# Stepping four side lanes of an RWKV-7 recurrence together at every eighth step of a projection stream, and storing another branch's gates first

## The chip, the cores and the metric

The kernel runs on one core of one Trainium2 chip. The metric is device time in microseconds (us) of one execution, the median of several runs. The engines are PE (TensorE: matmuls, and the weight loads that the profile lists as PEld), DVE (VectorE), ACT (ScalarE), POOL (GpSimd) and SP (SyncE, which here only issues DMAs). Each engine works through its own queue in order and waits on semaphores of the others.

## The reference

One decoder layer is computed for a prompt of 512 tokens and 8 samples of 8 tokens, 576 tokens in all, with a model width of 1024:

```
xn = RMSNorm(x)
proj = xn @ w_in            # 1024 x 13440: conv, rwkv, memory and gate columns
y_conv = B * conv3(C * h) * silu(g_conv)
y_rwkv = RWKV7(shifted r, k, v, decay, icl) * silu(g_rwkv)
y_mem  = softmax(q K_mem^T / sqrt(d)) V_mem * silu(g_mem)
merged = sum_i sigmoid(m_i) * (y_i @ w_branch_i)
y = RMSNorm_final(x + merged @ w_out)
```

The recurrence of RWKV-7 (16 heads with a state of 64 x 64) goes, step by step, as

```
sa = S kk
S  = S * w - sa (kk * a)^T + v k^T
o  = S r
```

and the layer also returns the memory keys and values and the new states.

## The kernel before

Everything is laid out with features on the 128 partitions and the 576 tokens in the free dimension, as two halves of 288. A weight tile of 1024 x 128 is loaded as two DMAs on SP, split by ACT (`wh`, L99) and POOL (`wl`, L93) into a high and a low part, and multiplied by the high and low parts of the activations. One such projection is 48 matmuls on L245, a pair for each of 24 steps. Its result stands in a PSUM tile `m`, of which there are two.

These projections are the **main stream**. It runs through 25 tiles for the recurrence's inputs, 32 for the convolution and 8 for the queries; then through gate tiles; and, after the recurrence, through the branch products (`w_br`) and what gates are left, and the output projection (L1284).

The recurrence runs beside it, on **side lanes**. A lane is a queue of Python generators. `drive` takes one step of the main stream (one pair of matmuls, here called a step), adds one to `TICK[0]`, and then steps each lane once, in the order chain, post, merge, invert, prepare. A generator that yields n is let alone for n steps and goes on at the next one. PE's order is the order in which this code issues (the pool is told so with `manual_schedule`), so a lane's step puts its matmuls between two pairs of the stream. The order on the other engines is set by the framework's scheduler.

The recurrence is done for eight pairs of heads, p = 0 to 7, in chunks of 64 tokens:

- `prep` (prepare lane) makes decays and scaled keys (L578, L579, L599), the chunk matrices (L633, L642), and at the end the bonus term (L676, L677). It yields 5, 5, 5, 3, 3, 5, 8, 6, 6 and 16 between its parts.
- `invert` (invert lane) solves a triangular system on DVE, two small operations per step for 31 steps, and writes it back over DRAM (`sco` to `msk`).
- `merge` (merge lane) transposes (L720, L727, L818, L819) and applies the inverse (L796, L803, L755, L756, L768), with yields of 4, 5, 5, 7, 5 and 6. It may go on from its first part only `READY` = 92 steps after the inversion.
- `chain` (chain lane) carries the state over the nine chunks (L869, L887, L882, L843), with a yield of 7 on either side of each half chunk.
- `post` (post lane) updates the samples' states (L916) and normalizes the output (L942, L946), with yields of 17, 1, 12 and 15.

All of these but the chain take their PSUM from one pool, tile name `s`, **with two buffers for all lanes** (`stile`, here called a slot). A slot is free again when ACT or DVE has read it out. `prep` takes two slots at once for L578/L579, for L633, for L642 and for L676/L677; merge takes two at L755/L756 and one elsewhere; post takes one at L916 and two at L942/L946.

The recurrence is longer than the work that the stream has for it. When convolution and queries are done, `filler` goes on with gate tiles of branches 1 and 2 (`EARLY`, L403), until all lanes are empty. Such a gate goes through tanh and is stored in DRAM (L506); `branch` later fetches it (L1018) in place of a projection. At the end of the program `prep_lane` loads and splits the output weights (`wout`) during branch 1, one eighth every 28 steps.

Of the kernel before, what the change touches and what calls it, by code (L numbers as in the profile page):

```python
# [17 lines left out]
TICK = [0]  # L18
# [67 lines left out]
def hybrid_step(ctx, tc, x_nat, x_t, mem_t, w_in, w_br, w_mk, w_mv, w_o, kc, vc, swkv,  # L86
# [5 lines left out]
    def tt(e, out, a, b, op):  # L92
        e.tensor_tensor(out=out, in0=a, in1=b, op=op)  # L93
# [4 lines left out]
    def act(out, in_, f=AF.Copy, **k):  # L98
        S.activation(out, in_, f, **k)  # L99
# [133 lines left out]
    def mm(src, rh=None, rl=None, n=HT, ps=None, parts=None):  # L233
        rh, rl = (xh, xl) if rh is None else (rh, rl)
        if parts is None:
            parts = wload(src.rearrange("p k f -> p (k f)"))
        nh = 1 if n == 256 else 2
        if ps is None:
            ps = pm.tile([128, 2, 512], F32, name="m")
        for k in range(8):  # L240
            h, l = parts[k // 4]
            f = slice(k % 4 * 128, k % 4 * 128 + 128)
            for i, (a, b) in enumerate(((h, rh), (h, rl), (l, rh))):
                for hf in range(nh):
                    TE.matmul(ps[:, hf, :n], a[:, f], b[:, k, hf * n:hf * n + n],  # L245
                              start=(k == 0 and i == 0), stop=(k == 7 and i == 2))
                if nh == 2 or i:
                    yield
        return ps
# [4 lines left out]

    class Lane:
        def __init__(self):
            self.q, self.cur, self.wait = [], None, 0

        def busy(self):
            return self.cur is not None or bool(self.q)  # L260
# [1 line left out]
        def step(self):  # L262
            if self.wait > 0:
                self.wait -= 1
                return
            if self.cur is None:
                if not self.q:
                    return
                self.cur = self.q.pop(0)
            try:  # L270
                self.wait = next(self.cur) or 0
            except StopIteration:
                self.cur, self.wait = None, 0

    chain_lane, post_lane, prep_lane, inv_lane, mrg_lane = (Lane() for _ in range(5))
    lanes = [chain_lane, post_lane, mrg_lane, inv_lane, prep_lane]

    def drive(main):
        for _ in main:
            TICK[0] += 1  # L280
            for ln in lanes:
                ln.step()
# [117 lines left out]
    def etile(tag, dt=F32, **k):  # L400
        return el.tile([128, T], dt, name="e" + tag, tag=tag, **k)

    EARLY = [(i, j) for i in (1, 2) for j in range(8)]  # L403
    gates = {}
    QT = ("r", "k", "A", "B", "C", "D", "E1", "F")
    qt = []
# [1 line left out]
    def queries():  # L408
        for j in range(8):
            ps = yield from mm(w_in[WQ + j])  # L410
            t = etile(QT[j])
            act(v3(t), m3(ps), scale=1.0 / 16)
            qt.append(t)
            yield "tile"

    with ExitStack() as rctx:
# [81 lines left out]
        def early_gates():  # L498
            for i, j in EARLY:
                ps = yield from mm(w_in[WM[i] + j])  # L500
                t = cvp.tile([128, T], F32, name="c")
                act(v3(t), m3(ps), AF.Tanh, scale=0.5)
                d = gates[i, j] = drp.tile([128, T], F32, name="gate%d%d" % (i, j), bufs=1)
                S.dma_start(out=d, in_=t)
                yield "tile"
# [9 lines left out]
        def lora():  # L515
            act(blkr, cc("blk"))
            ps = yield from mm(w_in[WP + 24])

            lor, swp = etile("A"), etile("B")
            shift(ps, 24, lor)  # L520
            act(lor[up], lor[up], AF.Tanh)
            S.dma_start(out=swp[dn], in_=lor[up])
            S.dma_start(out=swp[up], in_=lor[dn])
            stacks(lx, lor, swp)
            for o, (a, b) in enumerate(((lor, swp), (swp, lor))):
                tt(V, xlo[o][up], a[up], lx[o][up].bitcast(F32), ALU.subtract)
                tt(V, xlo[o][dn], b[dn], lx[o][dn].bitcast(F32), ALU.subtract)
# [25 lines left out]
        def proj(p, i):  # L553
            ps = yield from mm(w_in[WP + 8 * i + p])
            if i < 2:
                t = etile("rk"[i])
                shift(ps, 8 * i + p, t)
            else:
                t = fvas[p]
                shift(ps, 8 * i + p, t[:, :, 0, :], flat=False)  # L560
            got[p, i] = t
# [388 lines left out]
        def rwkv_main():  # L950
            yield from lora()
            n = [0, 0]

            def filler():
                es = early_gates()

                def one():
                    for x in es:
                        yield x
                        if x == "tile":  # L960
                            return
                    yield
                    yield "tile"

                for j in range(8):
                    while j >= 6 and want[0] < 8:
                        yield from one()
                    yield from conv(j)
                yield from queries()
                while any(ln.busy() for ln in lanes) or n[1] < 8:  # L970
                    yield from one()

            cg = filler()
            more = True
            while True:
                p = n[0] // 2
                if n[1] in fvas:
                    yield from proj(n[1], 2)
                    n[1] += 1
                elif p < 8 and want[0] >= p:  # L980
                    yield from proj(p, n[0] % 2)
                    n[0] += 1
                    if n[0] % 2 == 0:
                        prep_lane.q.append(prep(p))
                elif more:
                    more = False
                    for x in cg:
                        if x == "tile":
                            more = True
                            break  # L990
                        yield
                elif any(ln.busy() for ln in lanes) or n[1] < 8:
                    yield
                else:
                    return

        drive(rwkv_main())

    S.dma_start(out=o_conv, in_=cvo)
    S.dma_start(out=o_shift, in_=sho)  # L1000
# [13 lines left out]
    def branch(i, yh, yl, first=False, merged=None):  # L1014
        for j in range(8):
            if (i, j) in gates:
                th = etile("v", bufs=2)
                DMA.dma_start(out=th, in_=gates[i, j])  # L1018
            else:
                ps = yield from mm(w_in[WM[i] + j])  # L1020
                th = etile("v", bufs=2)
                act(v3(th), m3(ps), AF.Tanh, scale=0.5)
            ps = yield from mm(w_br[8 * i + j], yh, yl)
            if first:
                stt(v3(acc[:, j, :]), v3(th), 1.0, m3(ps), ALU.add, ALU.mult)
                continue
            stt(v3(th), v3(th), 1.0, m3(ps), ALU.add, ALU.mult)
            if merged is None:
                tt(G, acc[:, j, :], acc[:, j, :], th, ALU.add)
            else:  # L1030
                mgh, mgl = merged
                tt(G, th, acc[:, j, :], th, ALU.add)
                act(mgh[j], th, scale=0.5)
                stt(mgl[:, j, :], th, 0.5, mgh[j].bitcast(F32), ALU.mult, ALU.subtract)
# [204 lines left out]
    def wout(n, lag):  # L1239
        def place(pool, *parts):  # L1240
            r = []
            for tag, m in parts:
                t = pool.tile([128, m, 512], F32R, name="wo" + tag, tag=tag)
                r += [t[:, i, :] for i in range(m)]
            return r

        if n == 0:
            h, l = place(keep, *((t, 2) for t in SLOTS)), place(keep, ("s4", 7), ("s4b", 1))
        else:
            h, l = place(late, ("yh", 8)), place(late, ("yl", 8))  # L1250
        wo.append((h, l))
        for k in range(8):
            w = wp.tile([128, 512], F32, name="w", bufs=3)
            DMA.dma_start(out=w, in_=w_o[k, :, n * 512:n * 512 + 512])
            act(h[k], w)
            tt(G if k % 2 else V, l[k], w, h[k].bitcast(F32), ALU.subtract)
            yield lag


    prep_lane.q.append(wout(0, 27))  # L1260
    drive(branch(1, *parts, merged=(mgh, mgl)))
    for _ in wout(1, 0):
        pass
# [139 lines left out]
```

## Time and profile before

| what | us |
|---|---|
| median of 3 runs | 1235.94 (1234.75 to 1237.21) |
| the profiled execution: its own time | 1235.45 |
| its span, first to last instruction | 1233.6 |
| PE busy | 1186.9 (96%) |
| DVE, ACT, POOL busy | 587.0, 524.9, 573.8 |
| recurrence, 69 to 762 of the span | 693 |

The span is 1.85 us shorter than the execution's own time; the rest lies before the first and after the last instruction. PE is busy nearly throughout, but a busy PE is not a PE at its peak: ends of matmuls are modelled, so a matmul's time in the profile overlaps that of the next. Time between starts says more. Four stretches follow each other: memory keys and values with the norms (0 to 69), the recurrence beside the projections (69 to 762), attention beside branch 0 (762 to 910), the gates and branches 2 and 1 (910 to 1172), and the output projection.

### The profile page before, as it was taken

How to read it: one execution, taken by the hardware profiler on the slowest of the kernel's cores; microseconds unless marked ns; L12 is line 12 of the kernel's file. 1: busy time of each engine (PE TensorE's matmuls, PEld its weight loads, DVE VectorE, ACT ScalarE, POOL GpSimd, SP SyncE). 2: the span in 40 equal slices, each digit the busy share in tenths (PEclk: the TensorE clock that was granted, in tenths of full speed). 3: DMA queues.
4: the chain of work that ended last, by engine and by line, in shares of the span. 5: the costliest groups of instructions: out<-in, count | busy, mean ns of one | idle time of the engine just before them, and what ended most of it. 6: DMA issues, size and time to landing. Idle time of an engine off the chain costs nothing. (4 is left out here: it accounts for less than half of the span.)

```text
span 1233.6 us, 25594 instructions
## 1 busy us (share of the span) xinstructions
PE 1186.9 (96%) x10158; PEld 1100.8 (89%) x10158; DVE 587.0 (48%) x1514; ACT 524.9 (43%) x1120; POOL 573.8 (47%) x521
## 2 busy tenths in 40 slices
PE   7999979999899999999989999999999999999997
PEld 7798979989798988988879898889899999999976
DVE  7856866468675686647673315213113100134233
ACT  6563446435463544546344435333233222233222
POOL 4535532555535465454543545333334454446642
PEclk9999989999999999999999999999999999999999
DMA  8642222132321322222322225653632222225522
GB/s 290 213 126 72 70 72 63 59 91 58 91 65 53 89 68 84 90 86 70 110 80 74 69 71 171 195 181 123 208 97 87 80 84 86 78 86 161 161 105 78
DMA packets 93056, 129.39 MB, mean 105 GB/s; under 512 B 36988, under 2 KB 41320, under 8 KB 92936
## 3 DMA queue, kind: packets, MB, share of 16 engines
q1 hardware_dynamic: 55888, 110.20, 28.3%
q10 hardware_dynamic: 37048, 17.56, 5.4%
q8 instruction: 80, 1.31, 0.5%
q14 instruction: 40, 0.33, 0.1%
HBM read 115.96 MB, written 11.47 MB: 103 GB/s over the span
## 5 line engine op out<-in xcount | busy, mean ns | idle before, releaser
L93 POOL TENSOR_TENSOR wl<-w,wh 128x512 fp32r<-128x512 f32 x274 | 366.5, 1340 | 490.0 <-ACT wh L99 451.4
L245 PE MATMUL m<-xh,wh 128*128 128x288 f32 x1680 | 370.4, 302 | 0.5 <-ACT vst L99 0.5
L245 PE MATMUL m<-xl,wh 128*128 128x288 f32 x1680 | 369.4, 301 | 0.0
L245 PE MATMUL m<-xh,wl 128*128 128x288 f32 x1680 | 365.2, 299 | 0.0
L99 ACT ACTIVATE wh<-w 128x512 fp32r<-128x512 f32 x290 | 180.5, 627 | 294.2 <-PE m L245 169.1
L245 PEld LDWEIGHTS m<-xh,wh 128*128 128x128 f32 x1680 | 268.8, 189 | 8.6 <-issue 3.7
L245 PEld LDWEIGHTS m<-xl,wh 128*128 128x128 f32 x1680 | 269.2, 189 | 6.4 <-issue 2.9
L245 PEld LDWEIGHTS m<-xh,wl 128*128 128x128 f32 x1680 | 269.4, 189 | 3.0 <-issue 2.1
L96 DVE SCALAR_TENSOR_TENSOR ev<-ev,m 128x576 f32<-128x576 f32 x32 | 24.2, 755 | 168.4 <-PE m L245 110.3
L245 PE MATMUL m<-yh,wh 128*128 128x288 f32 x384 | 82.9, 297 | 0.0
L245 PE MATMUL m<-yh,wl 128*128 128x288 f32 x384 | 82.8, 297 | 0.0
L245 PE MATMUL m<-yl,wh 128*128 128x288 f32 x384 | 82.8, 297 | 0.0
L245 PEld LDWEIGHTS m<-yh,wl 128*128 128x128 f32 x384 | 61.7, 188 | 2.1 <-issue 2.1
L245 PEld LDWEIGHTS m<-yl,wh 128*128 128x128 f32 x384 | 61.7, 188 | 2.1 <-issue 2.1
L245 PEld LDWEIGHTS m<-yh,wh 128*128 128x128 f32 x384 | 61.7, 189 | 2.1 <-issue 2.1
L93 DVE TENSOR_TENSOR c<-c,tmp 108x84 f32<-108x84 f32 (+23 forms) x248 | 56.6, 228 | 5.4
L93 DVE TENSOR_TENSOR tmp<-c,nin 108x84 f32<-108x84 f32 (+23 forms) x248 | 54.8, 221 | 6.7 <-issue 1.2
L96 DVE SCALAR_TENSOR_TENSOR sb<-o,pcl,sb 64x64 f32<-64x64 f32 x112 | 31.6, 282 | 52.1 <-PE o L887 46.0
L99 ACT ACTIVATE osb<-o 64x128 f32<-64x128 f32 x72 | 19.7, 274 | 52.3 <-DVE sb L96 30.5
L93 DVE TENSOR_TENSOR vu<-o,vu 64x128 f32<-64x128 f32 x56 | 15.9, 284 | 46.6 <-PE o L869 45.6
L99 ACT ACTIVATE E<-m,par 128x32 f32<-128x32 f32 (+1 forms) x75 | 27.2, 418 | 22.2 <-PE m L245 14.1
L99 ACT ACTIVATE sb<-sb,pcl 128x128 f32<-128x128 f32 x56 | 22.5, 401 | 29.4 <-DVE sb L96 18.8
(441 smaller groups left out, 1796.2 us busy)
## 6 DMA issues: line engine op xcount, KB each, us to landing
w<-w_in_in SPq DMA_DIRECT2D x210, 256.0 KB
w<-w_br_in SPq DMA_DIRECT2D x48, 256.0 KB
kb<-kc_in SPq DMA_DIRECT2D x16, 512.0 KB
kb<-vc_in SPq DMA_DIRECT2D x16, 512.0 KB
w<-w_mk_in SPq DMA_DIRECT2D x16, 256.0 KB
w<-w_mv_in SPq DMA_DIRECT2D x16, 256.0 KB
w<-w_o_in SPq DMA_DIRECT2D x16, 256.0 KB
nin<-scr ACTq DMA_DIRECT2D x24, 144.0 KB
```

The costliest lines, as they stand in the source:

```text
L93: e.tensor_tensor(out=out, in0=a, in1=b, op=op)
L96: V.scalar_tensor_tensor(out=out, in0=a, scalar=s, in1=b, op0=op0, op1=op1)
L99: S.activation(out, in_, f, **k)
L245: TE.matmul(ps[:, hf, :n], a[:, f], b[:, k, hf * n:hf * n + n], start=(k == 0 and i == 0), stop=(k == 7 and i == 2))
```

## The change

Each lane gets a number `every`. A lane that is not counting down a yield goes on only at a step whose number is a multiple of `every`. For the recurrence alone, chain, post, merge and prepare lanes get 8; the invert lane keeps 1. A yield of 5 (the sixth step before) becomes the eighth step, 7 stays the eighth, 8 or 15 become the sixteenth, 16 or 17 the twenty-fourth. `EARLY` takes the gates of branch 2 before those of branch 1. The lag of `wout` is worked out from the number of tiles that branch 1 still has, at most 27.

```diff
     class Lane:
         def __init__(self):
-            self.q, self.cur, self.wait = [], None, 0
+            self.q, self.cur, self.wait, self.every = [], None, 0, 1
...
         def step(self):
             if self.wait > 0:
                 self.wait -= 1
+                return
+            if TICK[0] % self.every:
                 return
...
-    EARLY = [(i, j) for i in (1, 2) for j in range(8)]
+    EARLY = [(i, j) for i in (2, 1) for j in range(8)]
...
+        for ln in (chain_lane, post_lane, mrg_lane, prep_lane):
+            ln.every = 8
         drive(rwkv_main())
+        for ln in lanes:
+            ln.every = 1
...
-    prep_lane.q.append(wout(0, 27))
+    nt = 16 - sum((1, j) in gates for j in range(8))
+    prep_lane.q.append(wout(0, min(27, (24 * nt - 16) // 8 - 1)))
     drive(branch(1, *parts, merged=(mgh, mgl)))
```

The order on PE, at the place where the samples' state of the fifth pair of heads is updated. Before: prepare's L633, the chain's L869, and post's L916 with the merge lane's L768, L818 and L819 stand in three places, with pairs of the stream (L245) between them.

```order
L633 MATMUL s<-fva,fkb 128x128 x8
L245 MATMUL m<-xl,wh 128x288 x2
L869 MATMUL o<-sb,fva 128x128
L245 MATMUL m<-xh,wl 128x288 x2
L916 MATMUL s<-mb,chs 64x512
L916 MATMUL s<-mb_6933,chs 64x512
L768 MATMUL s<-yt,msk 64x64 x8
L818 MATMUL s<-idt,fkb 128x128
L819 MATMUL s<-idt,fva 128x128
L245 MATMUL m<-xh,wh 128x288 x2
```

Now, with line numbers higher by two (L871 is the chain's L869, L635 is prepare's L633):

```order
L245 MATMUL m<-xl,wh 128x288 x2
L871 MATMUL o<-sb,fva 128x128
L918 MATMUL s<-mb,chs 64x512
L918 MATMUL s<-mb_7244,chs 64x512
L770 MATMUL s<-yt,msk 64x64 x8
L820 MATMUL s<-idt,fkb 128x128
L821 MATMUL s<-idt,fva 128x128
L635 MATMUL s<-fva,fkb 128x128 x8
L245 MATMUL m<-xh,wl 128x288 x2
```

All four lanes stand in one place, and its matmuls take five slots in a row (L918 one, L770 one, L820 with L821 one, L635 two).

The order on SP's queue at branch 2. Before: gate weights (`w_in`) and branch weights (`w_br`) alternate.

```order
L224 DMA w<-w_in_in 128x512 x16
L224 DMA w<-w_br_in 128x512 x2
L224 DMA w<-w_in_in 128x512 x2
L224 DMA w<-w_br_in 128x512 x2
L224 DMA w<-w_in_in 128x512 x2
```

Now (`ev` is the tile that a stored gate is fetched into):

```order
L224 DMA w<-w_in_in 128x512 x14
L224 DMA w<-w_br_in 128x512 x5
L1025 DMA ev<-gate_5980 128x576
L224 DMA w<-w_br_in 128x512
L1025 DMA ev<-gate_6067 128x576
L224 DMA w<-w_br_in 128x512 x2
L1025 DMA ev<-gate_6314 128x576
```

The eight gates of branch 2 are fetched, and its gate projections are gone from there; they stand in the recurrence.

## Rows read from the trace of the kernel before

**Rows 1.** The page's line of busy time, share of the span and number of instructions, and its costliest group (line, engine, operation, tiles, shape and count; then busy us and mean ns of one; then idle us before and what ended it).

```profile
PE 1186.9 (96%) x10158; PEld 1100.8 (89%) x10158; DVE 587.0 (48%) x1514; ACT 524.9 (43%) x1120; POOL 573.8 (47%) x521
...
L245 PE MATMUL m<-xh,wh 128*128 128x288 f32 x1680 | 370.4, 302 | 0.5 <-ACT vst L99 0.5
```

**Rows 2.** Busy time of each engine in stretches of the span: the stretch and its length, then busy us and instructions of each engine, the granted clock, the DMA engines' busy share and GB/s.

```profile
core 0: us, PE busy (x) PEld busy (x) DVE busy (x) ACT busy (x) POOL busy (x), PEclk, DMA share, GB/s
69.00:762.00 693.00, 664.53 (x6428) 616.38 (x6429) 417.18 (x1245) 333.64 (x759) 340.78 (x331) 0.99 0.28 80
910.00:1172.00 262.00, 262.00 (x1968) 262.00 (x1967) 59.27 (x75) 81.69 (x136) 131.91 (x99) 1.00 0.33 101
```

**Rows 3.** What PE waited for in the recurrence, 69 to 762: who waited for whom, us in total, times, longest us.

```profile
engine line waited for: us in total, times, longest us
PE s L796 <- DVE ts L93: 5.5, 1, 5.5
PE s L633 <- DVE fkb L96: 2.6, 2, 1.4
PE o L869 <- DVE sb L96: 2.3, 3, 1.2
PE s L946 <- DVE chk L93: 2.0, 3, 0.7
PE o L869 <- ACT osb L99: 1.7, 2, 1.2
PE s L676 <- ACT gn L99: 1.7, 1, 1.7
PE s L676 <- DVE fva L761: 1.5, 2, 0.9
PE s L642 <- DVE msk L93: 1.4, 2, 1.0
PE s L916 <- DVE msk L93: 0.9, 1, 0.9
PE s L676 <- ACT vu L99: 0.8, 1, 0.8
PE s L803 <- ACT t L99: 0.8, 1, 0.8
PE s L578 <- ACT vu L99: 0.7, 2, 0.6
PE s L818 <- DVE S L93: 0.6, 3, 0.2
PE s L756 <- issue: 0.6, 1, 0.6
...
PE s L676 <- DVE ts4b L93: 0.5, 1, 0.5
PE o L882 <- DVE vu L93: 0.5, 1, 0.5
```

**Rows 4.** PE's instructions in order of time (start us, duration us, engine, line, tiles, shape, count) around one of the chain's L887 that stands alone between two pairs of the stream.

```profile
262.75 0.43 PE L245 MATMUL m<-xl,wh 128*128 128x288 f32 x2
263.02 0.38 PE L887 MATMUL o<-vu,chk 128*128 128x128 f32 x2
263.16 0.50 PE L245 MATMUL m<-xh,wl 128*128 128x288 f32 x2
263.50 0.42 PE L245 MATMUL m<-xh,wh 128*128 128x288 f32 x2
263.76 0.43 PE L245 MATMUL m<-xl,wh 128*128 128x288 f32 x2
```

**Rows 5.** The same view around one of prepare's L633 that stands alone.

```profile
310.23 0.42 PE L245 MATMUL m<-xh,wh 128*128 128x288 f32 x2
310.58 1.16 PE L633 MATMUL s<-fva,fkb 64*128 64x128 f32 x16
311.67 0.53 PE L245 MATMUL m<-xl,wh 128*128 128x288 f32 x2
312.04 0.42 PE L245 MATMUL m<-xh,wl 128*128 128x288 f32 x2
```

**Rows 6.** The same view where an L887 and an L633 stand together.

```profile
245.29 0.43 PE L245 MATMUL m<-xh,wl 128*128 128x288 f32 x2
245.55 0.39 PE L887 MATMUL o<-vu,chk 128*128 128x128 f32 x2
245.87 1.16 PE L633 MATMUL s<-fva,fkb 64*128 64x128 f32 x16
246.96 0.53 PE L245 MATMUL m<-xh,wh 128*128 128x288 f32 x2
247.33 0.42 PE L245 MATMUL m<-xl,wh 128*128 128x288 f32 x2
```

**Rows 7.** The same view where merge's L755 and L756 (two slots) and prepare's L676 (two more) stand together: the last of the one and the first of the other, with the idle time before it and its releaser.

```profile
481.61 0.22 PE L756 MATMUL s<-msk,vu 64*64 64x64 f32 x1
482.73 0.39 PE L676 MATMUL s<-eR,blkr 128*128 128x256 f32 x1 [0.90 <-DVE fva L761]
```

**Rows 8.** The fetches of stored gates, seven of them, on SP: issue time in ns (least, median, most), first and last start.

```profile
L1018 SPq DMA_DIRECT2D ev<-gate x7: 326/326/424, 1114.6 to 1151.6; - x7
```

## The prediction, made before the changed kernel ran

> **What bounds the kernel now.** I read the page's busy line first, then the stretches, then PE's waits, then its instructions one by one. The busy line has PE at 1186.9 us of a span of 1233.6 and no other engine above half [rows 1]. So time can go only by giving PE less to do, by making it wait less, or by letting the same matmuls follow each other faster. The stretches say where: from 910 to 1172, where the stream runs alone, PE is busy for 262.00 of 262.00 us, while in the recurrence it is busy for 664.53 of 693.00 [rows 2]. 28.5 us are idle there, and this is the stretch that the change touches. The column understates the waits. A stream matmul is shown with 302 ns [rows 1], but a pair of them follows the next pair after 0.26 to 0.27 us [rows 4], some 0.13 per matmul; so about 0.17 us of a wait that begins behind the stream hide under the modelled end.
>
> PE's waits in that stretch fall into two kinds [rows 3]. The first is a lane that waits for its own data: L796 5.5 us, once; L633 for `fkb` 2.6; L869 for the state 2.3 and for its bank's reader 1.7; L803 0.8; L756 0.6; L882 0.5. That is 14.0. The second is a lane that waits for one of the two slots, whose reader serves another lane or the same lane's other half: L946 2.0, L676 1.7, 1.5, 0.8 and 0.5, L642 1.4, L916 0.9, L578 0.7, L818 0.6, together 10.1. The rows sum to 24.1; the other 4.4 are small waits, which I count with the slots: 14.5.
>
> **What the change does not do.** The same matmuls run. The recurrence's stretch of the program goes from 72 tiles of 24 steps to 79, as 14 gates stand in it instead of 7; the same 7 gate tiles are gone from branches 2 and 1. Two gates are still left over for filling, so no step is empty: the longer recurrence costs PE nothing by itself. Seven more gates are stored and fetched; in branch 2 all eight products now follow each other with nothing but a fetch between. The trace has this pattern already, in branch 1: seven fetches of 326 ns each on SP [rows 8], inside a stretch in which PE has no idle time at all [rows 2]. I cost it at nothing; DVE and POOL, busy for 59 and 132 of those 262 us, hide the elementwise part. If that cover were gone, a product that waits for its weights would lose up to a few us at the start of branch 2; nothing here shows it. The lag of `wout` comes out as before: branch 1 has 10 tiles left, and (24 x 10 - 16) / 8 - 1 rounds down to 27.
>
> **Fewer interruptions.** In the program's order the stream is interrupted 276 times in the recurrence before, and 196 times now; the pieces of lanes' work are 352 in both. So 80 borders of a piece with the stream become borders with another piece. What is one worth? An L887 alone: from 262.75 to 263.50 there are two pairs and the L887, 0.75 us, less 2 x 0.265 leaves 0.22 [rows 4]. An L633 alone: 310.23 to 312.04 less two pairs, 1.28 [rows 5]. Both together: 245.29 to 247.33 less two pairs, 1.51 [rows 6], and 0.22 + 1.28 is 1.50. What is saved on the return to the stream (the first pair behind takes 0.34 to 0.37 us instead of 0.265) is paid between the pieces: the L887's two matmuls take 0.14 us up to the stream, but 0.32 up to the L633. So 80 x 0, and at most some 0.05 each where the shapes suit: -4 to +1, I take -1.
>
> This speaks against a rule that would favour the change. The Trainium skill (TensorEngine Tiling (Array Packing), Key Properties) says that changing the tiling mode drains TensorE. The changes of mode (128*128 to 64*128 and so on, counted in the order) go from 301 to 282; at an estimate of 0.1 us each, about the excess of that first pair, the rule gives -2 us where I take -1.
>
> **Waits for own data.** A step is 693.0 / 1728 = 0.40 us on average, at least 0.265. L633 now comes 16 steps after its inputs are issued instead of 9, 1.9 us later at least, and its longest wait was 1.4: -2.6. L803 and L756 get two more steps or one, 0.5 and 0.3: -0.8 of their 1.4. L796 comes 8 steps after the transposes instead of 5, and those start at a multiple of 8, 3.5 steps later on average: 6.5 x 0.40 = 2.6 of its 5.5. The chain's waits (4.5) stay, its steps being eight apart in both. Sum -6.0, with 0.17 hidden in each of five waits -7. Bounds: all 14.0 go, or the lanes' operations, issued together, queue on ACT and DVE and nothing goes.
>
> **Waits for slots.** Two opposite terms. Lanes now meet only within one step, and eight steps of stream, 2.1 us, lie between. A slot held for the usual 1 us or so (from the last L756 to the L676 that needed it 1.12 us passed [rows 7]) is free by then. Waits between interruptions go: 14.5 less the 3.4 that lie within one (next paragraph) is 11.1, plus 0.17 for each of some 12, -13.
>
> Within an interruption the pool is asked for more. Counting the slots that each takes, in the order: before, 6 interruptions want more than two, 8 slots too many in all; now 32 do, with 51 too many. What did the 8 cost? The three L676 behind L755/L756 or L727 waited 1.5, 0.5 and 0.8 us, the three L818 behind L916 and L768 together 0.6 [rows 3]: 3.4 us, 0.4 per slot. So 51 x 0.4 = 20.4, less 3.4, +17. Bounds: 0.2 per slot (the L818, where an L768 of other work stands between) gives +7; 0.9 (the longest L676) gives +43. I take 0.4, the mean, since the 51 are of both sorts.
>
> The Trainium skill (Perfetto Trace Analysis, Optimization Strategy) says that the same gap repeated on the engine that should be saturated can mean that there isn't enough PSUM for the next tile to be allocated. The 0.90 behind L756 [rows 7] is such a gap, and by this rule the change makes it the rule in each interruption; rival B is what that would be.
>
> **Sum.** -1 (interruptions) - 7 (data) - 13 (slots between) + 17 (slots within) = -4. From the profiled execution's 1235.45 that is 1231.5; that execution lies 0.5 below the median of the runs shown, so on the runs' scale 1232.
>
> **Rivals.**
> A, the forecast: the phases are sorted out, and slightly more waiting goes than comes. 1232, own range 1225 to 1234. Chance 0.40.
> B, the other side: two slots for four lanes that step together. In a cluster PE stands until ACT or DVE has read a slot that was filled just before. It decides from (1 + 7 + 13 + 3.4) / 51 = 0.48 us per slot. At 0.65, between the mean and the longest, it is 33 - 3.4 = +30, less 21, so +9: 1245. For it: the count of 51 against 8. Against it: in most of the 51 some PE work of another piece stands between filling and need. Chance 0.33.
> C: each of the 80 interruptions removed saves a whole return, 0.08 to 0.10 us, without the price between pieces: another -7, 1225. Against it stands the exact sum of rows 4 to 6; for it, that few pairs of pieces are as unlike as L887 and L633. Chance 0.07.
> D: gain and loss cancel to within 2.5 us. 1236. Chance 0.20.
> That the recurrence outgrows its filling would be a change that doesn't do what it says: each empty step 0.27 us. The count of 14 gates of 16 excludes it.
>
> **How the numbers follow.** A measurement of this kernel tells about 0.2%, 2.5 us, from no change. Faster: A without 0.03 at its edge towards no change, and C: 0.44. Same: D with that edge, less 0.01 at its slow end: 0.22. Slower: B and that end, 0.34. The range goes from 1219 (all 14.0 of the own-data waits gone, and C) to 1249 (0.73 us per slot).
>
> **What would show it.** Right: in the recurrence's stretch, now some 760 us long, L633's wait for `fkb` gone, L796's halved, and PE's waits within clusters (L635 behind L918 or L820, L580 behind L722 or L729, L678 behind L757) as the largest group, near 20 us in all; no idle time in branch 2. Wrong: those waits at 30 us or more, or chain waits (L871) grown above 4.5 because ACT and DVE get their work in bursts; or a first pair behind each cluster as short as a pair in the bare stream.

## The result, and the profile after

The changed kernel takes 1241.72 us (median of 6 runs, 1241.13 to 1247.72), the kernel before 1236.08 beside it: a ratio of 1.0058, 95% interval 1.0034 to 1.0082. It is slower by 5.6 us, where 4 us less were forecast. The profiled execution took 1247.04, the second longest of the six; a second profile of the same kernel (below) took 1243.35 and shows the same waits.

The page's busy line, as in [rows 1]:

```profile
PE 1191.8 (96%) x10158; PEld 1107.6 (89%) x10158; DVE 595.6 (48%) x1514; ACT 524.3 (42%) x1120; POOL 578.3 (46%) x521
```

The stretches, as in [rows 2]: the recurrence with its seven more gate tiles, and gates with branches 2 and 1.

```profile
core 0: us, PE busy (x) PEld busy (x) DVE busy (x) ACT busy (x) POOL busy (x), PEclk, DMA share, GB/s
70.50:819.30 748.80, 712.23 (x6761) 666.10 (x6762) 425.97 (x1238) 346.08 (x779) 363.13 (x345) 0.99 0.27 81
967.00:1183.60 216.60, 216.60 (x1627) 216.60 (x1626) 58.43 (x75) 68.50 (x114) 113.12 (x85) 1.00 0.37 116
```

PE is idle for 36.6 us in the recurrence instead of 28.5, and for none in branch 2: fetching its gates costs nothing, as forecast. So the loss lies in the recurrence. PE's waits there, as in [rows 3] (L580, L635, L644, L678, L770, L871, L884 are the lines 578, 633, 642, 676, 768, 869, 882 of before):

```profile
engine line waited for: us in total, times, longest us
PE s L580 <- ACT vu L99: 6.4, 5, 1.4
PE o L884 <- DVE vu L93: 4.2, 2, 3.2
PE s L580 <- ACT eA L99: 3.2, 4, 0.8
PE s L635 <- ACT chs L99: 2.4, 3, 1.4
PE s L678 <- DVE fva L763: 2.3, 4, 0.6
PE s L770 <- ACT gn L99: 2.3, 3, 0.8
PE o L871 <- ACT osb L99: 1.8, 2, 1.3
PE s L644 <- ACT yt L99: 1.7, 3, 0.6
PE s L635 <- DVE S L93: 1.7, 4, 0.5
PE s L678 <- DVE ts L93: 1.6, 3, 0.5
PE s L635 <- DVE fva L763: 1.5, 2, 0.9
PE s L580 <- ACT chs L99: 1.1, 3, 0.6
...
PE s L635 <- DVE msk L93: 0.8, 2, 0.7
...
PE s L820 <- DVE S L93: 0.6, 3, 0.2
```

L633's wait for `fkb` and L796's 5.5 us are gone, and so are L946's 2.0. Nearly all that is left stands on the tile `s`. The waits on `s` for a slot add up to 28.5 us, five smaller rows that are left out here included; before, some 14.5 us stood between and within interruptions. Of the 28.5, the 0.8 of `L635 <- msk` is a wait for slots that were filled in an earlier interruption. The other 27.7 us lie within interruptions, each behind slots that the same interruption had taken. The cluster shown with the change reads, in PE's instructions in order of time:

```profile
588.26 0.43 PE L245 MATMUL m<-xl,wh 128*128 128x288 f32 x2
588.53 0.38 PE L871 MATMUL o<-sb,fva 128*128 128x128 f32 x2
588.84 1.08 PE L918 MATMUL s<-mb,chs 128*64 128x512 f32 x4
589.85 0.68 PE L770 MATMUL s<-yt,msk 64*64 64x64 f32 x16
590.74 0.33 PE L820 MATMUL s<-idt,fkb 128*128 128x128 f32 x1 [0.21 <-DVE S L93]
590.90 0.27 PE L821 MATMUL s<-idt,fva 128*128 128x128 f32 x1
591.59 0.49 PE L635 MATMUL s<-fva,fkb 64*128 64x128 f32 x2 [0.41 <-ACT vu L99]
592.56 2.07 PE L635 MATMUL s<-fva,fkb 64*128 64x128 f32 x14 [0.48 <-ACT chs L99]
```

L918 and L770 take the two slots. L820 waits until DVE has read the first (`S`), the first L635 until ACT has read the second (`vu`), the next until ACT has read L820's (`chs`). The last row takes 2.07 us, and L633 alone took 1.16 [rows 5]. Here the granted clock plays a part:

```profile
200.00:203.40 3.40, 3.40 (x20) 3.12 (x18) 1.67 (x6) 1.61 (x3) 0.50 (x1) 0.50 0.01 2
264.90:268.30 3.40, 3.40 (x20) 3.18 (x21) 1.29 (x2) 0.00 (x0) 3.15 (x2) 0.50 0.51 152
312.70:316.10 3.40, 3.40 (x16) 3.40 (x15) 1.93 (x7) 0.55 (x2) 0.00 (x0) 0.51 0.04 10
432.10:435.50 3.40, 3.40 (x16) 3.36 (x15) 0.92 (x2) 0.63 (x1) 3.10 (x3) 0.50 0.27 77
592.50:595.90 3.40, 3.34 (x19) 3.12 (x20) 1.29 (x2) 0.00 (x1) 3.21 (x2) 0.51 0.46 144
```

These five stretches, 17.0 us, ran at 0.50, the 1.2 GHz level. Four came during or behind a cluster in which PE had stood, and the one at 312.7 behind the chain's longest wait:

```profile
311.78 0.68 PE L884 MATMUL o<-vu,msk 128*64 128x64 f32 x8 [3.17 <-DVE vu L93]
```

Before the change there were two such stretches in the recurrence, with 10.2 us:

```profile
112.60:116.00 3.40, 3.40 (x17) 3.40 (x16) 1.08 (x1) 0.62 (x1) 3.32 (x3) 0.51 0.27 43
167.30:174.10 6.80, 4.38 (x77) 3.98 (x77) 5.54 (x27) 3.23 (x10) 3.55 (x4) 0.50 0.26 81
```

At half speed at most half of such a stretch is lost, so the difference is at most 3.4 us.

This execution's span is 11.6 us longer than that of the one profiled before. Of these, 1.4 us lie ahead of the recurrence, in which the change does nothing; the granted clock was lower there too (before first, then now):

```profile
0.00:69.00 69.00, 58.68 (x342) 52.12 (x342) 55.63 (x88) 42.72 (x77) 31.89 (x31) 0.98 0.70 233
0.00:70.40 70.40, 60.58 (x342) 53.77 (x342) 55.66 (x88) 42.56 (x77) 31.46 (x31) 0.93 0.68 228
```

The other 10 us are 8.1 us more idle time in the recurrence, 1 us less of it beside branch 0, and some 3 us more busy time, no more than the half clock can have cost.

### The profile page after: what moved, and what is told of

Read it like the earlier page. It is cut to its first block, busy times and chain, and to the rows that moved or that the text cites. A ratio compares the mean times of both kernels' runs of the same rounds, so it can differ in the third digit from the quotient of the medians.

```text
span 1245.2 us, 25593 instructions
## 1 busy us (share of the span) xinstructions
PE 1191.8 (96%) x10158; PEld 1107.6 (89%) x10158; DVE 595.6 (48%) x1514; ACT 524.3 (42%) x1120; POOL 578.3 (46%) x521
## 3 DMA queue, kind: packets, MB, share of 16 engines
q1 hardware_dynamic: 56896, 112.26, 28.5%
## 4 chain that ended last, share of the span: by engine, by line
PE 79%; DVE 9%; issue 4%; ACT 3%; POOL 1%; DMA 1%; ACTq 0%; POOLq 0%; DVEq 0%
PE m L245 60%; PE m L1292 4%; PE s L1097 2%; PE s L635 2%; PE o L884 2%; PE o L889 1%; PE o L871 1%; DVE c L93 1%; PE s L770 1%; PE c L1167 1%; DVE eD L586 1%; DVE msk L93 1%; DVE tmp L93 1%; PE o L1200 1%; PE s L757 1%
## 5 line engine op out<-in xcount | busy, mean ns | idle before, releaser
L93 POOL TENSOR_TENSOR wl<-w,wh 128x512 fp32r<-128x512 f32 x274 | 370.4, 1355 | 483.0 <-ACT wh L99 454.0
L245 PE MATMUL m<-xh,wh 128*128 128x288 f32 x1680 | 367.7, 300 | 0.6 <-ACT vst L99 0.5
L245 PE MATMUL m<-xh,wl 128*128 128x288 f32 x1680 | 366.6, 300 | 1.4 <-POOL E L427 0.8
L245 PE MATMUL m<-xl,wh 128*128 128x288 f32 x1680 | 367.0, 300 | 0.0
L245 PEld LDWEIGHTS m<-xh,wl 128*128 128x128 f32 x1680 | 270.6, 190 | 6.3 <-issue 2.5
L245 PEld LDWEIGHTS m<-xh,wh 128*128 128x128 f32 x1680 | 270.2, 190 | 6.3 <-issue 2.1
L245 PEld LDWEIGHTS m<-xl,wh 128*128 128x128 f32 x1680 | 270.6, 190 | 4.7 <-issue 2.9
L245 PE MATMUL m<-yh,wh 128*128 128x288 f32 x384 | 82.9, 297 | 0.0
L245 PE MATMUL m<-yl,wh 128*128 128x288 f32 x384 | 82.8, 297 | 0.0
L245 PE MATMUL m<-yh,wl 128*128 128x288 f32 x384 | 82.7, 297 | 0.0
L245 PEld LDWEIGHTS m<-yl,wh 128*128 128x128 f32 x384 | 61.7, 188 | 2.1 <-issue 2.1
L245 PEld LDWEIGHTS m<-yh,wl 128*128 128x128 f32 x384 | 61.7, 188 | 2.1 <-issue 2.1
L245 PEld LDWEIGHTS m<-yh,wh 128*128 128x128 f32 x384 | 61.6, 188 | 2.1 <-issue 2.1
L93 DVE TENSOR_TENSOR msk<-s,con 128x512 f32<-128x512 f32 (+1 forms) x48 | 24.6, 551 | 31.0 <-PE s L635 26.5
```

## The experiments

One theory and three rivals were put against each other. **S**: the loss is the wait for two slots within clusters, some 28 us over 51 slots too many, 0.56 each in the expectations (0.54 without the row on `msk`). **B**: not the slots, but lanes that issue together queue on ACT and DVE. **G**: the moved gates cost. **I**: what counts is the number of interruptions, at 0.09 us each; it can't explain by itself that 80 fewer are slower, and is priced as a part of most placements below. All runs carry the changed order of the gates. In the runs with phases, `step` asks for `(TICK[0] - self.phase) % self.every`.

**Gates alone (e1_order_only).**

```diff
-            ln.every = 8
+            ln.every = 1
```

> The change without its main part: the lanes step at every step as before, and only the order of the stored gates (branch 2 first) and the lag of wout are new; 7 gates, 276 interruptions, 8 slots too many, as before. Theory S (the time of the change lies in the two PSUM slots that clusters ask too much of) and rival B (bursts on ACT and DVE): as before, 1236, ratio 0.998 to 1.002. Rival G (the moved gates cost at branch 2 or 1): slower by 3 to 6 us.

1235.65 us against 1235.04, ratio 1.0001 (0.9991 to 1.0012). G falls: here seven gates are stored, and in the change, with 14, the stretch of branch 2 shows no idle time. The effect is that of the eighth step.

**Prepare four steps apart (e2_prepare_apart).**

```diff
-        for ln in (chain_lane, post_lane, mrg_lane, prep_lane):
-            ln.every = 8
+        for ln, ph in zip((chain_lane, post_lane, mrg_lane, prep_lane), (0, 0, 0, 4)):
+            ln.every, ln.phase = 8, ph
```

> As the changed kernel, but the prepare lane steps four steps after the other three (phase 4 of 8). 235 interruptions instead of 196, 10 slots too many within one instead of 51, 14 gates as in the change. Theory S: the waits within clusters fall from about 28 us to about 6, some waits between interruptions come back (1.06 us of stream between the two phases): 1222 to 1230, faster than both. Rival B: the burst of prepare is taken out of the other lanes' step, about half of the loss: 1238 to 1240. Rival I (what counts is the number of interruptions, 0.09 us each): 39 more, 1245.

1223.44 us, ratio 0.9909 (0.9896 to 0.9922): faster than both, where S put it. The stretch of its recurrence and PE's longest waits in it:

```profile
69.70:794.90 725.20, 705.05 (x6760) 660.47 (x6761) 424.41 (x1238) 345.08 (x782) 363.47 (x345) 1.00 0.28 84
```

```profile
PE s L580 <- ACT eB L99: 2.5, 4, 0.6
PE s L770 <- ACT gn L99: 2.3, 3, 0.8
PE s L757 <- DVE msk L807: 1.6, 1, 1.6
...
PE o L871 <- ACT osb L99: 1.3, 1, 1.3
```

20.2 us idle instead of 36.6. L580's waits for `vu` and `chs` and L635's for `S` and `fva` are gone: these were prepare's slots held by merge and post. L770 behind post's `gn` stays, since post and merge still meet.

**All four apart (e3_all_apart).** The same with phases (0, 2, 4, 6).

> As the changed kernel, but the four lanes at phases 0, 2, 4 and 6 of 8: each still steps at every eighth step only, and never two together. 305 interruptions, no slot too many within one. Theory S: waits within clusters are gone (28 us), waits between lanes two steps apart (0.53 us, less than a slot is held) take a part of it back: 1225 to 1235. Rival I: 109 more interruptions at 0.09 us, 1251. Rival B: as before the change or somewhat better, 1234 to 1238.

1226.45 us, ratio 0.9929 (0.9914 to 0.9944), as S has it. The recurrence:

```profile
69.90:798.20 728.30, 710.75 (x6760) 660.87 (x6761) 426.67 (x1238) 346.41 (x781) 367.68 (x345) 1.00 0.28 83
```

Idle time is down to 17.6 us, and yet it is 3.0 us behind e2, with 70 more interruptions. PE is busy for 5.7 us more than in e2 (710.75 against 705.05), with the same matmuls and 6.8 us at the half clock in both. If all of that were the price of the 70, it would be 0.08 us each. So rival I's forecast of 1251 is out, and with it the number of interruptions as what decides; its price of 0.09 is not. Whether these 5.7 us are a price or waits hidden behind modelled ends, these runs don't separate.

**Three slots (e4_three_slots), and its control (e5_inversion_sbuf).** The inversion's PSUM bank is freed by keeping its tile in SBUF; e4 gives the bank to the lanes, e5 leaves out the new `stile`.

```diff
...
         def stile():
-            return psd.tile([128, 512], F32, name="s")
...
+            nst[0] += 1
+            return (psd.tile([128, 512], F32, name="s") if nst[0] % 3 else pch.tile([128, 512], F32, name="c"))
...
         def invert(p, msk, mu_, nin, sco, fkb, fva, pcl, rn):
+            zp = rw.tile([128, 352], F32, name="zp", bufs=1)
+            S.dma_start(out=zp[0:108], in_=const_d[0:108, NC1:NC1 + 352])
             yield 28
 
-            zp = pch.tile([128, 512], F32, name="c")
...
-            act(zp[0:108, 0:352], zini)
```

> As the changed kernel, but with three slots for the lanes: the inversion's tile is kept in SBUF instead of its PSUM bank, loaded by a DMA instead of a copy by ACT, and every third slot comes from that bank. Clusters as in the change (196 interruptions), 19 slots too many instead of 51. Theory S: waits within clusters fall from 28 us to about 11, 1222 to 1230. Rivals B, G and I: no slot is involved, 1240 to 1243 (what the inversion's tile in SBUF does by itself, a few us either way, is to be run alone).

> The control for e4_three_slots: the inversion's tile in SBUF as there, but two slots as in the change. In e4 the inversion's operations on DVE took 370 and 330 ns instead of 228 and 221, 248 of each, which makes some 60 us more of DVE in the recurrence. Theory S: two slots cost some 18 us more than three, 1290 to 1300. If slots do not matter (rivals B, I): the same as e4, 1278 to 1282.

e4 took 1279.76 us, ratio 1.0356 (1.0342 to 1.0369), a miss by 50 us: with its tile in SBUF the inversion is much slower. In e4's groups on DVE its two operations have

```profile
L93 DVE TENSOR_TENSOR zp<-zp,tmp 108x84 f32<-108x84 f32 (+23 forms) x248 | 91.6, 370 | 6.2
L93 DVE TENSOR_TENSOR tmp<-zp,nin 108x84 f32<-108x84 f32 (+23 forms) x248 | 81.8, 330 | 8.4 <-DMA nin<-scr 2.5
```

and had 228 and 221 ns in PSUM. Against its control it answers all the same: e5 took 1296.0, ratio 1.049 (1.0471 to 1.0509), so with the same clusters the third slot is worth 16 us where S said 18 and the others nothing. In e5's waits stand (its lines are numbered as before the change: L578 is the change's L580)

```profile
PE s L578 <- ACT vu L99: 10.3, 5, 2.9
...
PE s L676 <- DVE fva L761: 3.5, 4, 1.7
```

and neither of the two is among e4's rows beyond 0.3 us. Idle time in the recurrence is 68.3 us in e5 and 56.7 in e4, and the mean granted clock there 0.98 and 0.97, so the gain is not the clock's. The waits for slots are longer in e5 than in the change (10.3 us for `vu` instead of 6.4), so the 16 us hold for a kernel with this slower inversion and can't be carried over to the change.

**The chain apart (e6_chain_apart).** Phases (4, 0, 0, 0): the lane that takes hardly any slot is taken out of the clusters. (It does take one per pair of heads, at L843, now L845, against what the description of the kernel and the expectation say; the counts of 51 and 50 have it in.)

> As the changed kernel, but the chain, which takes no slot, steps four steps after the other three lanes: 271 interruptions (as many as before the change, 276), 50 slots too many within one (51 in the change). Theory S: the clusters still ask too much of the pool, with even less work between, 1240 to 1248. Rival B (bursts on ACT and DVE delay the chain): the chain has its own step, 1230 to 1236. Rival I: 75 more interruptions at 0.09 us, 1248.

1249.82 us, ratio 1.0124 (1.0108 to 1.014), slower than the change itself and a little above S's 1248. B falls: with a step of its own the chain waited more, not less.

```profile
PE s L580 <- ACT vu L99: 4.8, 5, 2.5
PE o L884 <- DVE vu L93: 4.7, 1, 4.7
PE o L871 <- ACT osb L99: 3.5, 1, 3.5
...
PE o L889 <- DVE vu L93: 2.6, 1, 2.6
```

The slots' rows stay. The chain's 10.8 us, against 6.3 in the change, lie on top; 20.4 us at the half clock against 13.6 in e7, and the price of 75 more interruptions, can have their part in the time. Rival I's 1248 fits this run as well as S's, so it speaks against B alone.

**The change once more (e7_changed_again).**

> The changed kernel once more, for its median beside the same runs and a second profile: 1241 to 1243; in the profile of the recurrence the same waits for slots, about 28 us.

1243.09 us, ratio 1.0064 (1.0046 to 1.0083). Its profiled execution, 1243.35, has the same rows on `s` within 0.4 us each, 35.7 us of idle time in the recurrence, and 13.6 us at the half clock instead of 17.0.

**Every fourth step (e8_every_fourth).** `every = 4`.

> As the changed kernel with every fourth step in place of every eighth: 243 interruptions, 24 slots too many within one, 11 gates. Theory S by count: 24 x 0.56 = 13 us of waits within clusters and lanes that meet 1.06 us apart, between e2_prepare_apart and the kernel before: 1228 to 1236. Rival I: 33 fewer interruptions than before, 1233. Rival B: 1238 to 1240.

1246.88 us, ratio 1.0103 (1.0087 to 1.0119): slower than the change, outside S's range by 11 us. Its waits begin with

```profile
PE o L871 <- DVE sb L96: 4.0, 2, 3.2
PE m L245 <- ACT wh L99: 3.6, 1, 3.6
PE o L871 <- ACT osb L99: 2.7, 3, 1.8
```

34.4 us are idle in the recurrence, 5.9 more than before the change. Counted by their places in the order, the waits behind slots too many are 14.0 us, close to S's 13. What S had not priced is that the chain waits 8.5 us, the stream itself 3.6 us for weights, once, and that five stretches, 20.4 us, ran at the half clock, which can have cost up to 5.1 us more than the 10.2 before. So the count held for the waits that it prices, and it did not give the time. Why the chain, the weights and the clock cost more at every fourth step stays open; B's 1238 to 1240 and I's 1233 lie too low as well.

**Two more placements.** e9_post_between has phases (0, 3, 0, 5), e10_post_prepare (0, 4, 0, 4), for chain, post, merge and prepare.

> As e2_prepare_apart, but in three groups: chain and merge at phase 0 of 8, post at 3, prepare at 5. 246 interruptions, one slot too many within one (10 in e2). Theory S by count alone: 4 to 5 us of waits within clusters less than e2, 1218 to 1221; but post now steps only 0.53 us ahead of prepare, and what e3_all_apart lost to e2 by short distances (3 us) may come back: up to 1225.

> Two groups again, but post goes with prepare (phase 4) and merge stays with the chain (phase 0): 240 interruptions, 7 slots too many within one. Theory S: post and merge no longer meet (3.4 us of waits of L770 for post's reader in e2), post and prepare do: 1220 to 1226. A measure of whether it is the number of slots or which pair of lanes meets: if the pair matters more than the count, outside that.

e9: 1222.03 us, ratio 0.9895 (0.9881 to 0.991). e10: 1223.46, ratio 0.9905 (0.9888 to 0.9921). Both lie within S's wider range, e9 a us above the 1218 to 1221 by count alone, and neither can be told from e2 by much. With fewer than about ten slots too many the count decides little here: what e9 saves behind slots too many (2.0 us against 5.8 in e2) comes back in the other waits on `s` (11.8 against 9.2). Of the 3.4 us that the expectation of e10 puts down to post's reader in e2, 2.3 (`gn`) are; the 1.1 for `yt` is merge waiting for its own data.

## Why the prediction was wrong

The result lies on the side of rival B, which had 0.33. The parts that it rested on, by its own steps:

- **Waits for slots, those within.** This step failed, by its price. The count of 51 against 8 was right, and so was the place; 0.4 us per slot was the mean of eight places before, and 27.7 / 51 = 0.54 came out. That is above the 0.48 at which the prediction itself had rival B begin, and 7 us more than the 20.4 in the sum. The eight held three L818 with 0.2, which have an L768 between filling and need. The costliest of the 51 have less between: L580's second half comes behind L729 and its own first half, and three times waits 1.4 us for ACT's read of L729's whole bank (`vu`). The prediction put its sign of being right near 20 us and that of being wrong at 30; 27.7 lies nearer to the second.
- **Waits for slots, those between.** Right but for one: of the waits with this cause only the 0.8 us of `L635 <- msk` is left. Of the 13 in the sum, 2 were estimated as hidden, and no row shows them.
- **Own data.** -7 was forecast. 14.0 us became 6.5 by the rows (4.2, 1.8, and two small ones), -7.5. But the total is right by luck: L796's 5.5 are gone wholly instead of by half, and the chain has 6.3 instead of 4.5, with one wait of 3.2 us. Chain waits above 4.5 were one of the prediction's signs of being wrong, by bursts of the lanes' work; ahead of this one, DVE stood for operations of POOL's (last section), and that the change brought this about is not shown.
- **Interruptions.** 80 x 0 could not be tested alone and stays open. By e2 and e3 an interruption could cost 0.08 us of busy time, at which 80 fewer would save 6 us. No such saving shows: PE's busy time in the recurrence grew by 47.7 us, of which the seven more gate tiles, by what branches 2 and 1 lost, are 45.4. Either the price is paid between pieces, as the prediction had it, or short waits hidden behind modelled ends took it back.
- **The half clock** was no term of the sum, and so at nothing without a reason. It is worth at most 3.4 us in the first profile and 1.7 in the second.
- **The gates** at nothing: right, by e1 and by a stretch of branch 2 without idle time.

The sum with what was measured: -12.2 (between) - 7.5 (own data) + 27.7 - 3.4 (within) = +4.6 for the waits, against -3 in the forecast without its interruptions; at most 1.7 to 3.4 us of half clock come on top. The median is +5.6. That the price of a slot is the cause rests on e2, e3, e9 and e10, which take the clusters apart and keep the eighth step and the gates, and on e4 against e5, which keep the clusters and add a slot. That the low clock follows from the stands in clusters is only argued from where it lies.

The larger lesson is that the change held a gain of some 12 us and spent it: a lane that steps only at every eighth step waits less for its own data and hardly ever meets another lane's slot from the step before. Putting all four lanes on the same eighth step gave that back.

## What to carry to other kernels

When side work is issued into a dense stream of matmuls, its distance to the next piece matters more than the number of interruptions: keep lanes that share a pool of PSUM buffers some steps apart (here prepare four steps from the rest, 1223 us against 1242). Before merging pieces, count how many buffers each merged place takes beyond the pool, and price each with the read-out of a full bank where nothing covers it, not with a mean over places where other work stood between; that price was not tried on another kernel. Such a count prices these waits alone: at every fourth step it gave them to within a us (14.0 against 13) and missed the time by 11.

## What the runs showed of the hardware that was not expected

DVE on SBUF can stand for the whole of an operation on POOL. In the changed kernel, ahead of the chain's longest wait, DVE shows

```profile
307.17 1.44 DVE L96 SCALAR_TENSOR_TENSOR ts3c<-U,par,ts3c 128x32 f32<-128x32 f32 x1
...
308.69 1.14 DVE L96 SCALAR_TENSOR_TENSOR ts3c<-U,par,ts3c 128x32 f32<-128x32 f32 x1
...
310.71 0.24 DVE L96 SCALAR_TENSOR_TENSOR ts3c<-U,par,ts3c 128x32 f32<-128x32 f32 x1
```

and POOL

```profile
307.12 1.44 POOL L93 TENSOR_TENSOR fva<-er,eC 128x576 f32<-128x576 f32 x1
308.52 1.26 POOL L93 TENSOR_TENSOR wl<-w,wh 128x512 fp32r<-128x512 f32 x1
```

The same operation on 128x32 takes 0.24 us with POOL idle, and ends with POOL's operation where the two meet. The Trainium skill (SBUF — State Buffer, Terms) calls this a pair of ports that DVE and GpSimd share, held by one for a full instruction; the trace agrees. The inversion of e4, with both operands in SBUF, shows the same. Of its 496 operations 64 took longer than 0.45 us, and each of these ended within 0.12 us behind an operation of POOL's; the 382 that met no operation of POOL's took 225 ns on average. In the change, with one operand in PSUM, none of the 496 took longer than 0.45 us.
